# Two attention stages: units in the order D D G G D M, and the projections' steps spread over them by a table of their TensorE time

## The chip, the cores and the metric

The kernel runs on one core of a Trainium2 chip. The metric is the device time of one execution in microseconds (us); the kernel before took 2622.73 us in the median of three runs (2622.46 to 2626.35).

## The reference

Eight stages follow each other on a sequence of 512 tokens with 1024 features, all in float32: two attention blocks (`first_block`, layers 0 and 1), and then a block of four gated feed-forward stages around a state space mixer and a convolution mixer. The change touches the attention blocks only. One layer of them computes

```python
h = rms_norm(x, pre_norm[l])
proj = h @ w_in[l]     # split into dq dk dv dgate, gq gk gv ggate, mq mgate
oa = diff_attention(rope(dq), rope(dk), dv, lam)     # 6 heads, two softmaxes each: p1 - lam * p2
oa = rms_norm(oa, diff_subln[l]) * (1 - lambda_init) * silu(dgate)
ob = gqa_attention(rope(norm(gq)), rope(norm(gk)), gv) * silu(ggate)     # 6 heads on 2 key heads
mk, mv = split(rms_norm(mem, mem_norm[l]) @ w_mem_kv[l])
om = softmax(mq @ mk.T / 8) @ mv * silu(mgate)     # 4 heads on 256 memory rows
x = x + rms_norm(concat(oa, ob, om) @ w_out[l], post_norm[l])
```

## The kernel before

Every float32 product of the projections is made of three passes on TensorE (`mm3`, lines 160 to 164): high by high, high by low, low by high, where `splith` (lines 166 to 170) makes the high part by a copy on ACT and the low part by a subtraction on DVE. Weights come by DMA into a `raw` tile (line 144); `load` makes their high part on ACT (line 151) or DVE (149) and their low part on DVE or POOL (156). Of twelve weight tiles in a row, eight have their low part made on POOL and four both parts on DVE. In attention the high and low tiles are taken from a pool `w` of 13 tiles, two for each load.

**Units.** Attention itself (`attn`) is a list of 40 units. A D unit is one block of 128 queries of one differential head with its two softmaxes: 24 of them in three groups D0, D1, D2 of two heads by four blocks. A G unit is two blocks of queries of a grouped head: 12 in two groups G0, G1 of three heads by two. An M unit is a whole memory head: 4. For a unit, PE makes the scores (`unit_scores`, line 566 for D, 574 for G, 583 for M), DVE takes two maxima (line 556), ACT makes two exponentials with their sums (558), in a D unit DVE combines both softmaxes (the mix, lines 592 to 594), PE transposes the result (`unit_turn`, line 618, four matmuls for each block of queries, 606 in M), ACT copies it out as the high part (619), DVE makes the low part (`unit_low`, 624), and PE multiplies by the values (`unit_av`, 641 and 642). `unit_out` folds and stores a finished head (652 to 688).

**Steps.** The projections come in chunks. `chunk_d` makes queries, keys and values of two D heads, `chunk_g` those of three G heads, `chunk_gate` (T0 to T3) a quarter of the gates, `chunk_mkv` (KV) the memory's keys and values and `chunk_mq` (MQ) the memory queries. A chunk loads its weights and then yields in steps. A D step is 24 matmuls of 384 columns for one block of tokens, a G step 24 of 320, an MQ step 24 of 256, a step of a gate 48 of 256 (two blocks), a KV step 24 of 512. After its matmuls a D step issues the rope on DVE and POOL, two splits and, one step later, eight transposes (line 394); a G step has a norm with a square and a power on POOL (464, 186) and the lines 466, 471, 473 and 475 on DVE.

**The order around the change.** D0 is projected ahead of all units. The loop over the units (end of `attn`) issues for unit i: the scores of i + 2, the exponentials of i + 1, the low part of i - 1, the mix and transposes of i, the values of i - 1, the output of i - 2. Steps of the chunks are issued in between by three helpers: `starts(i)` issues the first half of each step whose time has come, `ends()` the other half, and `need(i)` issues whatever is left of every chunk up to one that is due. When a step's time comes is told by the list `fill` in `DEFAULT`, with a first unit and a distance in units for each chunk; the order of the groups is the string `order`. From this text a scheduler makes each engine's queue when the program is built: it may take a later instruction first where an earlier one would not be ready by its reckoning. On the chip each engine runs its queue in order.

SBUF tiles are taken from pools by name (`BUFS`, with `ALIAS`). Queries and keys (`dqk`, `gq`, `mk`, `mq`, `memT`) and the two tiles of transposed probabilities (`pt`) share the pool `u8` of six with tiles of other stages.

## Time and profile before

| | before |
|---|---|
| median of three runs | 2622.73 us (2622.46 to 2626.35) |
| the profiled execution | 2622.51 us, span 2620.7 us |
| PE busy | 2529.3 us (97%) |
| DVE, ACT, POOL busy | 1456.7 us (56%), 1045.6 us (40%), 672.3 us (26%) |
| mean granted clock of TensorE | 0.989 |
| attention, layer 0: first unit's work to the last | about 62 to 312 us |
| attention, layer 1 | about 406 to 653 us |

The span is the time from the first to the last instruction. A busy PE is not PE at its peak, since a matmul's duration covers its way through the array and the next one starts before it ends. The granted clock is 1.00 where TensorE runs at the higher of its two levels (2.4 GHz) and 0.50 where it runs at the lower (1.2 GHz). Transposes of line 618 mark the pace of the units: one block of four matmuls for a D unit, two for a G unit.

### The profile page before, as it was taken

How to read it: one execution, taken by the hardware profiler on the slowest of the kernel's cores; microseconds unless marked ns; L12 is line 12 of the kernel's file. 1: busy time of each engine (PE TensorE's matmuls, PEld its weight loads, DVE VectorE, ACT ScalarE, POOL GpSimd, SP SyncE). 2: the span in 40 equal slices, each digit the busy share in tenths (PEclk: the TensorE clock that was granted, in tenths of full speed). 3: DMA queues.
4: the chain of work that ended last, by engine and by line, in shares of the span. 5: the costliest groups of instructions: out<-in, count | busy, mean ns of one | idle time of the engine just before them, and what ended most of it. 6: DMA issues, size and time to landing. Idle time of an engine off the chain costs nothing.

```text
span 2620.7 us, 34611 instructions
## 1 busy us (share of the span) xinstructions
PE 2529.3 (97%) x13503; PEld 2180.6 (83%) x13503; DVE 1456.7 (56%) x2309; ACT 1045.6 (40%) x1964; POOL 672.3 (26%) x887
## 2 busy tenths in 40 slices
PE   7998999989999999989999999999999998999998
PEld 7997889978888788888888888888888876888887
DVE  6777667786478952488433332533323797533322
ACT  5457645576334442323433322433323434433321
POOL 5543245543135620223200000200002781300000
PEclk9999999999999999999999999999999999999999
DMA  4211142112234542543222223222222211222221
GB/s 158 67 52 61 55 155 70 61 57 79 75 102 185 189 171 104 184 162 114 97 97 97 97 98 105 96 97 97 98 98 85 98 64 41 104 90 97 101 92 65
DMA packets 68899, 262.81 MB, mean 100 GB/s; under 512 B 7936, under 2 KB 8448, under 8 KB 64384
## 3 DMA queue, kind: packets, MB, share of 16 engines
q1 hardware_dynamic: 68736, 260.61, 28.4%
q8 instruction: 106, 1.74, 0.3%
q14 instruction: 57, 0.47, 0.1%
HBM read 239.61 MB, written 20.97 MB: 99 GB/s over the span
## 4 chain that ended last, share of the span: by engine, by line
PE 50%; DVE 4%; POOL 1%; issue 1%; ACT 0%; DVEq 0%; POOLq 0%; ACTq 0%
PE t L163 16%; PE t L164 16%; PE t L162 16%; DVE t L1250 1%; POOL t L156 1%; DVE t L156 0%; DVE t L209 0%; PE t L217 0%; DVE t L241 0%; PE t L1106 0%; ACT t L203 0%; PE t L1275 0%; PE t L1105 0%; PE t L1104 0%; DVE t L170 0%
## 5 line engine op out<-in xcount | busy, mean ns | idle before, releaser
L162 PE MATMUL t<-t,t 128*128 128x512 f32 (+2 forms) x3593 | 1304.2, 365 | 12.3 <-ACT t L169 4.8
L163 PE MATMUL t<-t,t 128*128 128x512 f32 (+2 forms) x3593 | 1303.9, 363 | 6.0 <-POOL t L1229 3.4
L164 PE MATMUL t<-t,t 128*128 128x512 f32 (+2 forms) x3593 | 1302.4, 363 | 1.5 <-DVE t L170 1.3
L156 DVE TENSOR_TENSOR t<-t,t 128x1024 fp32r<-128x1024 f32 (+2 forms) x318 | 399.2, 1258 | 695.0 <-PE t L163 608.8
L162 PEld LDWEIGHTS t<-t,t 128*128 128x128 f32 x3593 | 678.4, 189 | 118.5 <-ACT t L169 9.9
L163 PEld LDWEIGHTS t<-t,t 128*128 128x128 f32 x3593 | 680.2, 189 | 108.3 <-POOL t L1229 4.2
L164 PEld LDWEIGHTS t<-t,t 128*128 128x128 f32 x3593 | 679.8, 189 | 102.0 <-DVE t L170 3.3
L151 ACT ACTIVATE t<-t 128x1024 fp32r<-128x1024 f32 (+2 forms) x370 | 386.5, 1048 | 678.5 <-PE t L164 591.5
L156 POOL TENSOR_TENSOR t<-t,t 128x512 fp32r<-128x512 f32 (+4 forms) x98 | 179.4, 1847 | 692.2 <-PE t L163 635.8
L170 DVE TENSOR_TENSOR t<-t,t 128x512 fp32r<-128x512 f32 (+3 forms) x316 | 193.6, 631 | 141.3 <-ACT t L169 140.8
L169 ACT ACTIVATE t<-t 128x512 fp32r<-128x512 f32 (+3 forms) x316 | 155.6, 517 | 249.2 <-DVE t L300 98.7
L299 ACT ACTIVATE t<-t 128x512 f32<-128x512 f32 x88 | 52.5, 597 | 217.6 <-PE t L164 215.0
L558 ACT ACTIVATE t<-t,t 128x512 f32<-128x512 f32 (+1 forms) x176 | 114.1, 658 | 37.1 <-DVE t L556 35.0
L238 POOL TENSOR_SCALAR t<-t,t 128x1 f32<-128x1 f32 x32 | 12.0, 375 | 424.8 <-ACT t L235 420.0
L556 DVE TENSOR_REDUCE t<-t 128x1 f32<-128x512 f32 (+1 forms) x160 | 106.1, 681 | 14.7 <-PE t L574 8.7
L1250 DVE SCALAR_TENSOR_TENSOR t<-t,t,t 128x512 f32<-128x512 f32 x136 | 95.5, 750 | 11.3 <-PE t L164 9.6
L624 DVE TENSOR_TENSOR t<-t,t 128x512 fp32r<-128x512 f32 x112 | 76.1, 685 | 42.0 <-ACT t L619 34.8
L1204 POOL TENSOR_TENSOR t<-t,t 128x1024 fp32r<-128x1024 f32 (+5 forms) x12 | 18.9, 1577 | 236.3 <-DVE t L170 236.3
L961 POOL TENSOR_TENSOR t<-t,t 128x64 f32<-128x64 f32 (+3 forms) x112 | 65.2, 601 | 54.6 <-DVE t L890 46.8
L209 DVE SCALAR_TENSOR_TENSOR t<-t,t,t 128x512 f32<-128x512 f32 x72 | 55.7, 815 | 40.7 <-POOL t L186 40.5
L979 DVE TENSOR_TENSOR t<-t,t 128x256 f32<-128x256 f32 x128 | 65.4, 574 | 12.7 <-DMA t<-in_s5bc 12.4
L186 POOL TENSOR_TENSOR t<-t,t 128x1 f32<-128x1 f32 (+2 forms) x98 | 69.5, 711 | 7.0
(220 smaller groups left out, 2235.5 us busy)
## 6 DMA issues: line engine op xcount, KB each, us to landing
t<-in_W SPq DMA_DIRECT2D x356, 512.0 KB, 3.5
mats<-t SPq DMA_DIRECT2D x16, 1024.0 KB, 4.9
t<-mats SPq DMA_DIRECT2D x16, 1024.0 KB, 5.5
t<-in_gv SPq DMA_DIRECT2D x19, 512.0 KB, 4.1
t<-in_W SPq DMA_DIRECT2D x24, 384.0 KB, 3.2
t<-in_W SPq DMA_DIRECT2D x8, 480.0 KB, 3.5
t<-in_x SPq DMA_DIRECT2D x4, 512.0 KB, 7.1
t<-in_mem SPq DMA_DIRECT2D x4, 512.0 KB, 3.8
```

Source lines behind the costliest of these rows:

```text
L151: nc.scalar.activation(h[:, :c], raw[:, :c], AF.Copy)
L156: eng.tensor_tensor(out=l[:, o:o + m], in0=raw[:, o:o + m], in1=h[:, o:o + m].bitcast(F32), op=ALU.subtract)
L162: mm(out, lhs[0], rhs[0], start=start, stop=False)
L163: mm(out, lhs[0], rhs[1], start=False, stop=False)
L164: mm(out, lhs[1], rhs[0], start=False, stop=stop)
L169: nc.scalar.activation(h, src, AF.Copy)
L170: nc.vector.tensor_tensor(out=l, in0=src, in1=h.bitcast(F32), op=ALU.subtract)
L186: self.nc.gpsimd.tensor_tensor(out=r, in0=r, in1=self.mh.to_broadcast([P, n]), op=ALU.pow)
L556: v.tensor_reduce(out=mx[:, q * w:q * w + w], in_=part, axis=AX.X, op=ALU.max, negate=True)
L558: act.activation(e[:, i], part[:, i - q * w], AF.Exp, bias=mx[:, i:i + 1], accum_out=u["d"][:, i:i + 1])
L624: v.tensor_tensor(out=lo, in0=tp, in1=h.bitcast(F32), op=ALU.subtract)
L1250: v.scalar_tensor_tensor(out=pc, in0=z[:, i:i + 512], scalar=cp[:, f, 5 + i:6 + i], in1=pc, op0=ALU.mult, op1=ALU.add)
```

## The change

The units go D0, D1, G0, G1, D2, M. The list `fill` is now an order of chunks, and when a step's time comes is worked out: `room` says how much TensorE time a unit of each kind leaves free, `STEPS` how many steps a chunk has and how long one is on TensorE, and a step is put at the first unit by whose end the free time exceeds the time of the steps ahead of it. T3 goes from the first place to the last. Queries and keys get a pool of their own (`a8`, five tiles), so do the two tiles `pt`, and `w` falls from 13 to 10 tiles.

```diff
-DEFAULT = {"pool": [0, 1, 3, 4, 6, 7, 9, 10], "hv": [2, 5, 8, 11], "after": [], "order": "DGDGDM", "fill": [["T3", 55.0, 2], ["T0", 8, 0.5], ["D1", 15, 1.5], ["G0", 3, 1.5], ["T1", 25.0, 2], ["G1", 4, 2], ["T2", 0, 1], ["D2", 15.0, 1], ["KV", 28.0, 1], ["MQ", 29.0, 2]]}
+DEFAULT = {"pool": [0, 1, 3, 4, 6, 7, 9, 10], "hv": [2, 5, 8, 11], "after": [], "order": "DDGGDM", "fill": "T0 D1 G0 T1 G1 T2 D2 KV MQ T3", "room": {"D": 4.1, "G": 2.5, "M": 2.5}}
+
+STEPS = {"D": (4, 4.2), "G": (4, 3.5), "T": (2, 5.8), "KV": (2, 5.5), "MQ": (4, 2.9)}
...
-    BUFS = {"u2": 6, "u4": 10, "u8": 6, "w": 13, "wf": 11, "raw": 3,
+    BUFS = {"u2": 6, "u4": 10, "u8": 6, "a8": 5, "pt": 2, "w": 10, "wf": 11, "raw": 3,
...
-    ALIAS = {k: "u4" for k in "gcs dv dst gk gst mt mv mst e gain xn xs rot cy z".split()} | {k: "u2" for k in "t1 y0 junk sg gg cb tmp su pbc pmt dbl tap".split()} | {k: "u8" for k in "dqk gq memT mk mq pt p8 mat z2 dg zz".split()}
+    ALIAS = {k: "u4" for k in "gcs dv dst gk gst mt mv mst e gain xn xs rot cy z".split()} | {k: "u2" for k in "t1 y0 junk sg gg cb tmp su pbc pmt dbl tap".split()} | {k: "u8" for k in "p8 mat z2 dg zz".split()} | {k: "a8" for k in "dqk gq memT mk mq".split()}
...
-        fill = [dict(at=max(at, start.get(nm, -1)), by=by, due=due[nm], after=start.get(nm, -1), gen=chunks[nm]) for nm, at, by in PRM["fill"]]
+        room, have = [], 0.0
+        for u in units:
+            have += PRM["room"][u["id"][0]]
+            room.append(have)
+        fill, took = [], 0.0
+        for nm in PRM["fill"].split():
+            steps, cost = STEPS[nm if nm in STEPS else nm[0]]
+            ats = []
+            for k in range(steps + 1):
+                ats.append(next((i for i in range(n) if room[i] > took), n))
+                took += cost if k < steps else 0.0
+            fill.append(dict(ats=[max(a, start.get(nm, -1)) for a in ats], due=due[nm], after=start.get(nm, -1), gen=chunks[nm]))
...
-            while fill and fill[0]["at"] <= i:
+            while fill and fill[0]["ats"][0] <= i:
                 ends()
-                if fill and fill[0]["at"] <= i:
-                    fill[0]["at"] += fill[0]["by"]
+                if fill and fill[0]["ats"][0] <= i:
+                    if len(fill[0]["ats"]) > 1:
+                        fill[0]["ats"].pop(0)
                     advance(fill[0], 0)
```

In the program's text, ahead of the scheduler, the steps move as follows. Before: T3 and T0 whole at unit 5, D1 and G0 whole at unit 6, T1, G1 and T2 at units 11 and 12, D2 at 15 to 19, KV at 28 to 30, MQ at 30 to 34. Now: T0 at units 0 to 2, D1 at 2 to 6, G0 at 6 to 10, T1 at 10 to 12, G1 at 13 to 16, T2 at 16 to 20, D2 at 21 to 26, KV at 28 to 30, MQ at 30 to 33, T3 at 33 to 36.

What the scheduler makes of it is read from the queues. A row names the line, the operation, the tile written and those read, and the size written; line numbers of the change are two higher in this part of the code. Three places of layer 0 follow.

**D0's units 6 and 7.** PE, before: the transposes of D0's unit 6 (tile 1374) with what stands behind them. Lines 162 to 164 with 320 columns are a step of G1.

```order
L163 MATMUL t_1768<-t_1712,t_63 128x320
L164 MATMUL t_1768<-t_1711,t_63 128x320
L162 MATMUL t_1768<-t_1717,t_63 128x320
L618 MATMUL t_1374<-t_64,t_845 128x128 x4
L163 MATMUL t_1768<-t_1718,t_63 128x320
L574 MATMUL t_1355<-t_1111,t_1110 128x512 x2
L574 MATMUL t_1356<-t_1111,t_1110 128x512 x2
L574 MATMUL t_1389<-t_1111,t_1110 128x512 x2
L164 MATMUL t_1768<-t_1717,t_63 128x320
L162 MATMUL t_1768<-t_1717,t_63 128x320
```

PE now: the transposes of unit 6 (tile 1011) and of unit 7 (tile 1100), which read the mix of unit 7.

```order
L166 MATMUL t_1303<-t_1043,t_63 128x320
L396 MATMUL t_988<-t_63,t_977 128x128 x4
L620 MATMUL t_1011<-t_64,t_857 128x128 x4
L568 MATMUL t_994<-t_671,t_670 128x512
L568 MATMUL t_995<-t_671,t_670 128x512
L568 MATMUL t_1060<-t_671,t_670 128x512
L568 MATMUL t_1061<-t_671,t_670 128x512
L568 MATMUL t_1130<-t_671,t_670 128x512
L620 MATMUL t_1100<-t_64,t_999 128x128 x4
L643 MATMUL t_1017<-t_459,t_214 128x256
```

DVE now, at the same place: the low part of unit 6 (line 626), then what stands ahead of the mix of unit 7 (line 596, tile 999).

```order
L626 TENSOR_TENSOR t_460<-t_1011,t_459 128x4x128
L558 TENSOR_REDUCE t_1066<-t_994 128x1
L558 TENSOR_REDUCE t_1066<-t_995 128x1
L468 TENSOR_REDUCE t_1090<-t_1084 128x4
L594 RECIPROCAL t_1095<-t_856 128x1
L558 TENSOR_REDUCE t_1136<-t_1060 128x1
L595 SCALAR_TENSOR_TENSOR t_1095<-t_856,t_1095,t_64 128x1
L558 TENSOR_REDUCE t_1136<-t_1061 128x1
L596 SCALAR_TENSOR_TENSOR t_999<-t_999,t_1095 128x512
L473 TENSOR_TENSOR t_1085<-t_1085,t_1092 128x256
```

Steps of projections stood around unit 6's transposes; now five score matmuls stand between the transposes of units 6 and 7, and eight rows of DVE between the low part of the one and the end of the mix of the other.

**G units.** PE, before, in G1's units (28 to 39 of the blocks of transposes): transposes, scores and values, with no step among them.

```order
L618 MATMUL t_2731<-t_64,t_2661 128x128 x4
L641 MATMUL t_2771<-t_459,t_1702 128x256
L574 MATMUL t_2711<-t_1701,t_1700 128x512 x2
L618 MATMUL t_2759<-t_64,t_2717 128x128 x4
L574 MATMUL t_2745<-t_1701,t_1700 128x512 x2
L618 MATMUL t_2765<-t_64,t_2717 128x128 x4
L642 MATMUL t_2771<-t_460,t_1702 128x256
```

PE now, in G1's units: a step of D2 (384 columns).

```order
L576 MATMUL t_2381<-t_1614,t_1613 128x512 x2
L165 MATMUL t_2517<-t_2303,t_63 128x384
L166 MATMUL t_2517<-t_2302,t_63 128x384
L164 MATMUL t_2517<-t_2302,t_63 128x384
L657 MATMUL t_2275<-t_64,t_2273 128x64 x4
L643 MATMUL t_2264<-t_459,t_1028 128x256
L576 MATMUL t_2445<-t_1614,t_1613 128x512 x2
L165 MATMUL t_2517<-t_2303,t_63 128x384
L576 MATMUL t_2446<-t_1614,t_1613 128x512
L620 MATMUL t_2360<-t_64,t_2244 128x128 x4
```

D2's later steps went from the second D group into the G units; they stand in one bunch of five blocks of transposes, and the blocks ahead of it and behind it have no step.

**The last D units and M.** PE, before: the last transposes of D2 (tile 3443) and M's first (line 606).

```order
L618 MATMUL t_3443<-t_64,t_3391 128x128 x4
L583 MATMUL t_3449<-t_2957,t_3134 128x256 x4
L583 MATMUL t_3450<-t_2957,t_3134 128x256 x4
L606 MATMUL t_3477<-t_64,t_3429 128x128 x4
L641 MATMUL t_3409<-t_459,t_2209 128x256
L583 MATMUL t_3489<-t_2957,t_3134 128x256 x4
```

PE now: the last transposes of D2 (tile 3391) and the start of T3's second step, 48 matmuls, all ahead of M's first transposes.

```order
L585 MATMUL t_3367<-t_2841,t_3018 128x256 x4
L620 MATMUL t_3391<-t_64,t_3312 128x128 x4
L164 MATMUL t_3397<-t_3266,t_63 128x256
L165 MATMUL t_3397<-t_3267,t_63 128x256
L166 MATMUL t_3397<-t_3266,t_63 128x256
L164 MATMUL t_3397<-t_3266,t_63 128x256
```

T3 stood ahead of T0, at the start of the stage.

## Rows read from the trace of the kernel before

**Rows 1.** Windows of the two attention stages: start:end, length, busy us (instructions) of PE, PEld, DVE, ACT, POOL, then granted clock, DMA share, GB/s.

```profile
62.00:312.00 250.00, 232.79 (x1643) 216.75 (x1641) 192.91 (x362) 157.26 (x387) 105.75 (x153) 0.98 0.19 63
406.00:653.00 247.00, 229.75 (x1593) 212.91 (x1592) 191.26 (x358) 158.95 (x388) 112.26 (x155) 0.97 0.19 66
```

**Rows 2.** The same view, cut at the groups of units (eight of layer 0, three of layer 1).

```profile
62.00:135.00 73.00, 71.04 (x526) 70.21 (x525) 54.03 (x96) 35.83 (x89) 38.18 (x50) 1.00 0.23 74
135.00:159.00 24.00, 21.66 (x146) 19.59 (x144) 15.45 (x27) 14.94 (x34) 9.12 (x12) 1.00 0.20 66
159.00:205.00 46.00, 44.17 (x314) 42.52 (x311) 42.87 (x90) 27.84 (x75) 26.08 (x36) 1.00 0.14 47
205.00:225.00 20.00, 15.87 (x102) 13.88 (x103) 15.50 (x30) 15.03 (x35) 8.64 (x16) 0.83 0.22 67
225.00:247.00 22.00, 19.84 (x141) 17.06 (x139) 17.07 (x31) 18.44 (x45) 5.54 (x9) 1.00 0.21 72
247.00:270.00 23.00, 20.75 (x113) 16.95 (x113) 18.15 (x32) 13.19 (x28) 5.09 (x8) 0.93 0.14 46
270.00:297.00 27.00, 25.00 (x199) 23.13 (x197) 20.78 (x41) 20.77 (x54) 7.39 (x14) 1.00 0.28 94
297.00:312.00 15.00, 14.48 (x117) 13.43 (x115) 9.07 (x20) 11.22 (x32) 5.71 (x10) 1.00 0.00 1
544.00:563.00 19.00, 15.65 (x99) 13.03 (x100) 14.97 (x31) 14.73 (x34) 7.82 (x13) 0.82 0.22 84
585.00:610.00 25.00, 22.98 (x120) 18.81 (x120) 18.49 (x32) 13.57 (x29) 5.09 (x8) 0.86 0.14 46
636.00:653.00 17.00, 14.82 (x103) 13.46 (x104) 9.60 (x20) 14.88 (x43) 11.12 (x15) 0.90 0.25 94
```

**Rows 3.** The same view for the transposes of line 618 alone (PE, PEld).

```profile
225.00:247.00 22.00, 6.99 (x48) 5.65 (x47) 1.00 0.21 72
```

**Rows 4.** Groups of lines on DVE, 50 to 320 us: form xcount | busy us, mean ns | idle before.

```profile
L556 DVE TENSOR_REDUCE t<-t 128x1 f32<-128x512 f32 x72 | 47.9, 681 | 10.3 <-PE t L574 6.0 <-PE t L566 4.1
L624 DVE TENSOR_TENSOR t<-t,t 128x512 fp32r<-128x512 f32 x56 | 38.0, 684 | 19.7 <-ACT t L619 16.4 <-ACT t L611 3.0
L594 DVE SCALAR_TENSOR_TENSOR t<-t,t 128x512 f32<-128x512 f32 x24 | 20.5, 854 | 0.4
L593 DVE SCALAR_TENSOR_TENSOR t<-t,t,t 128x1 f32<-128x1 f32 x24 | 5.7, 239 | 0.2
L592 DVE RECIPROCAL t<-t 128x1 f32<-128x1 f32 x24 | 3.6, 152 | 0.0
L466 DVE TENSOR_REDUCE t<-t 128x4 f32<-128x256 f32 x8 | 3.3, 409 | 1.2 <-POOL t L464 1.2
L156 DVE TENSOR_TENSOR t<-t,t 128x1024 fp32r<-128x1024 f32 x9 | 11.5, 1280 | 1.4 <-PE t L163 1.4
```

**Rows 5.** The same view on ACT.

```profile
L558 ACT ACTIVATE t<-t,t 128x512 f32<-128x512 f32 x72 | 49.5, 692 | 20.7 <-DVE t L556 19.1 <-DVE t L592 1.6
L619 ACT ACTIVATE t<-t 128x512 fp32r<-128x512 f32 x48 | 28.5, 600 | 11.6 <-PE t L618 11.5
```

**Rows 6.** Line 594 (the mix of a D unit) in the whole run: ns minimum/median/maximum.

```profile
L594 DVE SCALAR_TENSOR_TENSOR t<-t,t x48: 724/751/2295, 58.4 to 633.2; 128x512 f32<-128x512 f32 x48
```

**Rows 7.** The timeline of PE: start, us, instruction (two that follow each other).

```profile
60.32 0.28 PE L162 MATMUL t<-t,t 128*128 128x256 f32 x1
60.44 0.28 PE L163 MATMUL t<-t,t 128*128 128x256 f32 x1
```

**Rows 8.** Waits of PE from 205 to 225 us: total us, times, longest.

```profile
PE t L618 <- ACT t L558: 1.9, 1, 1.9
PE t L618 <- DVE t L624: 1.5, 1, 1.5
PE t L618 <- DVE t L664: 1.4, 1, 1.4
```

**Rows 9.** Groups of lines on POOL, 50 to 320 us.

```profile
L156 POOL TENSOR_TENSOR t<-t,t 128x1024 fp32r<-128x1024 f32 x7 | 17.4, 2492 | 0.1
```

## The prediction

> **What bounds the kernel now.** The windows of the two attention stages come first [rows 1]: in 250 us of layer 0 and 247 us of layer 1 PE is busy for 232.8 and 229.8 us, so it idles 17.2 us in each, and its granted clock averages 0.98 and 0.97. The program outside attention is the same before and after, so what the change can win lies in these two stretches. Cut at the groups of units [rows 2], the reader is to see where that idle time stands. While a pile of projection matmuls is at hand (62 to 135 us) PE idles 2.0 us of 73. It idles 2.3 us of 24 in the first G group, 1.8 us of 46 in the second D group, 4.1 us of 20 at that group's end, 2.2 us of 22 in the second G group, 2.3 us at the start of KV, 2.0 and 0.5 us in the last D group and in M. Where PE idles long its clock falls too: 0.83 from 205 to 225 us and 0.93 from 247 to 270 us in layer 0, 0.82, 0.86 and 0.90 in the three windows shown of layer 1. A clock share lost is PE time lost: 0.17 of 15.9 us is 2.7 us, 0.07 of 20.8 is 1.5, and in layer 1 0.18 of 15.7 is 2.8, 0.14 of 23.0 is 3.2, 0.10 of 14.8 is 1.5. Idle time and clock together are 34.5 + 11.7 = 46 us: more than that the change can hardly win.
>
> Next, what ends the idle time. From 205 to 225 us the waits are those of the transposes of line 618, for an exponential on ACT and for line 624 and 664 on DVE [rows 8]. At that place the PE queue has no projection matmul left, and the units run at the pace of their chain: scores, two maxima on DVE, two exponentials on ACT, in a D unit the mix on DVE, the transposes, the copy on ACT, the low part on DVE. The group costs of that chain are the rows on DVE and ACT [rows 4, 5].
>
> **The change, part by part.** The instructions stay the same; their order and three pool sizes change. So the sum is of waits that go and waits that come, and each is taken from a stretch of the trace in which units run with or without steps beside them.
>
> *The hole at the end of the second D group goes.* In the old order the steps of G1, T2 and D2 are used up when the last units of D1 are at work, and 4.1 us of idle time and 2.7 us of clock are lost there; in layer 1 it is 19 - 15.65 = 3.35 and 2.8 us [rows 2]. In the new order the second D group ends beside G1 and T2, whose matmuls stand around its last transposes. Both holes go: -13.0 us. Nothing worse than before can be hidden in that term, since what is late next at this place is PE itself.
>
> *G units.* Without steps beside them, 225 to 247 us, 48 transposes [rows 3] are 6 G units (8 each), and they lose 2.16 us of idle time, 0.36 a unit. In the old order both G groups lose 2.34 + 2.16 = 4.5 us. In the new order of PE, 9 of the 12 G units still have no projection matmul between their transposes: the scheduler takes T2 and D2 in two bunches, early and around the ninth unit. So 9 x 0.36 = 3.2 us stay, and 1.3 us a layer go: -2.5 us for both.
>
> *D units: new waits.* Here the change costs. D0 and D1 now follow each other, with T0, D1, G0, T1 and G1 beside them. At two places of the new order PE has next to nothing between the transposes of two D units. The first is shown above: between the transposes of D0's units 6 and 7 stand five score matmuls. DVE has to do, from the low part of unit 6 to the mix of unit 7, line 624 (0.684), four maxima (4 x 0.681), line 466 (0.409), the two small ones (0.152 and 0.239) and the mix (0.854): 5.06 us [rows 4]. Ahead of the low part go four transposes (6.99 / 48 = 0.146 each, 0.58 us [rows 3]) and the copy on ACT (0.600 [rows 5]). From transposes to transposes that is 6.2 us. PE's own work in it is the transposes and five score matmuls of 512 columns. Two 256-column matmuls start 0.12 us apart [rows 7], so I estimate 0.24 us for 512 columns and 1.8 us in all. PE waits 6.2 - 1.8 = 4.4 us. The second place, before unit 14, has the same list with a second line 466 and a sum of squares of about that size (5.9 us), less work of PE (transposes, two pairs of score matmuls, eight matmuls of line 641 and 642, four of line 655: some 2.9 us): 7.1 - 2.9 = 4.2 us. Around units 2 and 8 the same count leaves 0.8 and 0.5 us. So 10 us a layer come, and the 2.0 + 1.8 = 3.8 us that the two D groups lose now go with their old order: +6.2 us a layer, taken twice +12.5 us. The ends of this term: nothing at all (DVE runs ahead, and PE finds its work done: -3.8 x 2 = -7.6 us), and DVE slowed, which is the rival below.
>
> *T3 moves from the pile into the last D group.* Its 96 matmuls (4 blocks of rows, 8 slices, 3 products) are 96 x 0.12 = 11.5 us of PE [rows 7]. In the old order they stand ahead of T0, where PE is busy throughout, so they cost 11.5 us there; in the new order they stand beside D2's last units and before M's second unit. That stretch loses 2.0 + 0.5 us now, and in layer 1 2.2 us of idle time and 1.5 us of clock in its M part alone [rows 2]. Of these 6.2 us I take 5 to be filled, as M's last units still have nothing beside them: -5 us. Its ends are 0 and -6.2.
>
> *KV's start.* PE waits there for the norm of the memory (lines 203 to 217), which stays. Its clock loss, 1.5 and 3.2 us, follows on the lean stretch ahead; with D2's steps nearer I take 2 us of 4.7 as gone: -2 us, between 0 and -4.7.
>
> *Pools.* Weight buffers fall from 13 to 10 tiles (5 pairs). Where a chunk of 4 pairs follows another, only one pair is loaded ahead, and the next waits for its copy and its subtraction: 1.28 us on DVE, 2.49 us on POOL [rows 4, 9]. Units' matmuls and the last step of the chunk in front (24 x 0.12 us and more) stand beside it, so I take 0. If the cover is gone, the nine changes of chunk cost up to 2.49 us each where POOL does it. SP only issues the loads earlier or later; three raw buffers are unchanged. The separate pool for queries and keys has five tiles, and five is what D0, D1 and G0 hold at once, so I take 0 there.
>
> **Sum.** -13.0 - 2.5 + 12.5 - 5 - 2 = -10 us. The profiled execution took 2622.5 us, 0.2 us under the median of the three runs; the forecast is **2613 us**, with 2605 to 2621 as the forecast's own range from the ends of the last two terms and some us at either side for the count of the new waits.
>
> **A rule that speaks against it.** The mix reads two tiles in SBUF. It takes 0.751 us in the median and up to 2.295 us [rows 6], and POOL's subtractions of weights, 2.49 us each [rows 9], run beside the D units. The Trainium skill, page "SBUF — State Buffer", section "SBUF: two separate sides", says that a DVE operation with two SBUF inputs and a GpSimd operation exclude each other for a whole instruction. The longest mix agrees with that [rows 6]; by the rule alone each of the 9 subtractions that POOL makes in the new D groups of a layer could hold up a mix, and the sum would turn positive.
>
> **The rivals.**
>
> *All of it wins.* If the new waits in the D groups do not come (DVE does the maxima before the transposes need them), the term of +12.5 becomes -7.6, and the sum is -30 us: 2592. For it: from 62 to 135 us D units with steps beside them lose only 2.0 us. Against it: DVE was busy for 54 of 73 us there and for 42.9 of 46 from 159 to 205 us [rows 2], so it has little to run ahead with. 0.22.
>
> *Slower: POOL holds up the mix.* 9 of the 14 weight tiles of T0, D1, G0, T1 and G1 have their subtraction on POOL. If 8 of them in a layer meet a mix of the 16 D units, and each makes it 2.295 instead of 0.854 us, that is 8 x 1.44 = 11.5 us on the path from unit to unit, 23 us in both layers: -10 + 23 = +13, 2636 us. It decides once more than 4 mixes of a layer are hit where PE has no step to put beside them. For it: two D groups in a row with steps all through. Against it: the mean of the mix, 0.854, is only 0.1 us over its median, so about one in fifteen is hit now. 0.17.
>
> *No change.* The holes go, but as much comes back: the scheduler fills PE's queue with whatever is ready, in either order, so idle time only moves. Then -13.0 against +12.5 and the rest near nothing: 2622. For it: the bunches in the new order are as dense as in the old. Against it: T3's 11.5 us do move to a leaner place. 0.16.
>
> **The numbers.** The forecast has 0.45, of which 0.33 are faster by over 0.2%, 0.11 within it and 0.01 slower; 0.2% (5 us) is about what a measurement of this kernel can tell from no change. With the first rival faster has 0.55; with 0.12 of "no change", the same has 0.23; with the second rival and the 0.04 left of the third, slower has 0.22. The range reaches from the first rival to the second, 2592 to 2636 us; the few us beyond for weight buffers and for still slower mixes are the part left out.
>
> **What would show it.** In the profile after: the window at the end of the second D group has no low clock, and its waits for line 624 are gone (first term); PE waits some 4 us each for DVE ahead of line 620's transposes twice in the D groups of each layer (third term); M's and the last D group's windows idle less (fourth). Wrong would be: a D stretch whose idle time is below 4 us a layer (first rival), or mixes at 2 us in numbers (second).

## The result, and the profile of the changed kernel

The changed kernel takes **2660.45 us** in the median of four runs (2659.98 to 2665.21), the kernel before 2624.54 (2622.46 to 2627.53): a ratio of 1.0139, 95% interval 1.0124 to 1.0154. It is slower by some 36 us. The forecast was 2613 us with a range of 2592 to 2636: the sign was wrong and the time lies outside the range. The profiled execution of the changed kernel took 2665.2 us, the longest of the four, and that of the kernel before 2622.5; so the two traces differ by 42.7 us, some 7 more than the medians, and that much of what follows is the scatter of single executions.

| | before | after |
|---|---|---|
| span of the profiled execution | 2620.7 us | 2663.4 us |
| PE busy | 2529.3 us | 2545.0 us |
| DVE, ACT, POOL busy | 1456.7, 1045.6, 672.3 us | 1457.2, 1043.2, 672.5 us |
| mean granted clock | 0.989 | 0.980 |

DVE, ACT and POOL did the same work in the same time. PE is busy 16 us longer for the same matmuls (the lower clock) and idle 27 us longer. Line numbers of the changed kernel are two higher than before in this part.

The windows of the changed kernel, cut at its groups of units (columns as in [rows 1]): of layer 0, D0 and D1 from 64 to 180 us in five pieces, G0 and most of G1 to 226, the end of G1 to 251, the start of KV to 275, D2 to 311, M to 326; then the same ten of layer 1.

```profile
64.00:104.00 40.00, 39.03 (x257) 37.13 (x255) 28.67 (x59) 24.03 (x58) 21.50 (x28) 0.96 0.15 47
104.00:120.00 16.00, 9.96 (x48) 8.14 (x47) 13.32 (x28) 6.31 (x19) 7.39 (x12) 0.68 0.26 92
120.00:150.00 30.00, 30.00 (x229) 29.36 (x227) 23.06 (x47) 16.30 (x43) 17.30 (x26) 1.00 0.09 27
150.00:173.00 23.00, 17.67 (x115) 15.17 (x115) 18.25 (x41) 10.54 (x31) 17.80 (x27) 0.93 0.18 63
173.00:180.00 7.00, 7.00 (x58) 6.78 (x57) 4.08 (x10) 6.35 (x17) 3.23 (x5) 1.00 0.01 2
180.00:226.00 46.00, 43.46 (x289) 39.99 (x287) 31.02 (x57) 29.12 (x71) 13.78 (x17) 1.00 0.10 34
226.00:251.00 25.00, 19.05 (x131) 16.47 (x130) 16.76 (x30) 15.20 (x35) 6.32 (x7) 0.86 0.40 140
251.00:275.00 24.00, 21.31 (x120) 17.71 (x119) 18.12 (x31) 14.48 (x31) 9.24 (x10) 0.93 0.08 26
275.00:311.00 36.00, 34.55 (x292) 34.08 (x291) 25.09 (x43) 23.76 (x63) 6.84 (x15) 1.00 0.21 72
311.00:326.00 15.00, 13.73 (x108) 12.41 (x107) 9.83 (x21) 10.37 (x24) 5.66 (x9) 1.00 0.29 106
...
425.00:466.00 41.00, 37.44 (x257) 35.90 (x256) 30.73 (x57) 23.24 (x56) 18.58 (x26) 1.00 0.15 54
466.00:479.00 13.00, 8.73 (x49) 7.32 (x48) 10.74 (x26) 6.87 (x19) 9.32 (x13) 0.87 0.34 113
479.00:510.00 31.00, 31.00 (x238) 30.49 (x237) 23.42 (x50) 17.73 (x48) 19.54 (x28) 1.00 0.09 27
510.00:535.00 25.00, 18.41 (x114) 15.91 (x113) 17.06 (x41) 9.55 (x28) 16.27 (x25) 0.86 0.17 56
535.00:541.00 6.00, 6.00 (x49) 5.80 (x48) 3.90 (x10) 4.98 (x14) 3.22 (x5) 1.00 0.02 4
541.00:588.00 47.00, 44.48 (x297) 40.99 (x296) 31.41 (x57) 29.48 (x70) 12.39 (x16) 1.00 0.08 29
588.00:614.00 26.00, 19.25 (x126) 17.27 (x126) 16.31 (x29) 16.26 (x36) 5.52 (x8) 0.80 0.37 133
614.00:636.00 22.00, 19.49 (x113) 15.97 (x112) 17.63 (x29) 13.01 (x29) 8.43 (x10) 1.00 0.00 1
636.00:675.00 39.00, 36.98 (x298) 36.24 (x297) 26.07 (x46) 24.91 (x64) 7.72 (x15) 0.96 0.23 82
675.00:690.00 15.00, 14.14 (x114) 13.04 (x113) 10.32 (x21) 10.52 (x24) 5.49 (x9) 1.00 0.30 107
```

Read each row as the prediction did: length less PE's busy time is idle time, one minus the clock times the busy time is what the clock lost. The steps were meant to be even, and PE's queue is not: from 120 to 150 us PE has no gap at all, on either side of it PE idles 6.0 us of 16 at a clock of 0.68 and 5.3 of 23 at 0.93. The two D groups lose 18.3 us in layer 0 (2.5, 9.2, 0, 6.6, 0) and 18.1 in layer 1 (3.6, 5.4, 0, 9.2, 0). The second place is new as well: the end of G1 (226 to 251 and 588 to 614 us) loses 8.6 and 10.6 us, where the second G group lost about 2 [rows 2].

As to length, layer 0 takes 264 us (62 to 326) against 250, layer 1 takes 266 (424 to 690) against 247, the stretch between them 98 against 94, and what follows 1973.4 against 1967.7.

What PE waited for, in the two D groups of layer 0 (62 to 180 us; total, times, longest), and then what DVE waited for from 62 to 323 us:

```profile
PE t L620 <- DVE t L596: 5.2, 2, 3.2
PE t L568 <- DVE t L626: 1.6, 1, 1.6
...
DVE t L151 <- PE t L165: 5.4, 1, 5.4
DVE t L424 <- PE t L166: 4.8, 1, 4.8
```

The first row is the wait the prediction had named: PE ahead of the transposes, for the mix, at units 7 and 14 (3.2 and 2.0 us). In layer 1's D groups it comes once, 2.0 us. In the last two rows DVE itself stands idle at the head of its queue, with work of a step that waits for PE's projection matmuls: the cast of a weight tile ahead of unit 7, and the rope at 187 us, in G0. Before, the cast waited 0.5 us at most in layer 0, and the rope 1.2 us, in layer 1 3.2. The timeline around unit 7 shows both sides (start, us, instruction, idle time before it and what ended it):

```profile
103.63 0.63 PE L620 MATMUL t<-t,t 128*128 128x128 f32 x4
104.67 1.19 PE L568 MATMUL t<-t,t 128*128 128x512 f32 x4 [0.40 <-ACT t L397]
107.44 0.50 PE L568 MATMUL t<-t,t 128*128 128x512 f32 x1 [1.59 <-DVE t L626]
111.10 1.08 PE L620 MATMUL t<-t,t 128*128 128x128 f32 x4 [3.16 <-DVE t L596]
...
115.32 0.41 PE L164 MATMUL t<-t,t 128*128 128x256 f32 x1
115.53 0.41 PE L165 MATMUL t<-t,t 128*128 128x256 f32 x1
...
102.51 1.84 DVE L151 CAST t<-t 128x960 fp32r<-128x960 f32 x1 [5.39 <-PE t L165]
104.46 2.33 DVE L158 TENSOR_TENSOR t<-t,t 128x960 fp32r<-128x960 f32 x1
106.71 0.68 DVE L626 TENSOR_TENSOR t<-t,t 128x512 fp32r<-128x512 f32 x1
107.31 1.27 DVE L558 TENSOR_REDUCE t<-t 128x1 f32<-128x512 f32 x2
110.22 0.74 DVE L596 SCALAR_TENSOR_TENSOR t<-t,t 128x512 f32<-128x512 f32 x1
...
101.57 2.27 POOL L158 TENSOR_TENSOR t<-t,t 128x960 fp32r<-128x960 f32 x1 [3.01 <-ACT t L153]
104.21 1.57 POOL L158 TENSOR_TENSOR t<-t,t 128x640 fp32r<-128x640 f32 x1 [0.37 <-ACT t L153]
```

PE ends its run of projection matmuls at 103.5 us; DVE has waited 5.4 us for that run, and then has a cast and a subtraction of weights to do (102.51 to 106.8) before the low part of unit 6, the maxima and the mix of unit 7. In that time PE has five score matmuls. The two engines take turns instead of working side by side. Behind the wait PE's matmuls of 256 columns start 0.21 us apart (115.32 and 115.53), before 0.12 [rows 7]: the granted clock stands at its lower level there.

### The profile page after: what moved, and what is told of

Read it like the earlier page. It is cut to its first block, busy times and chain, and to the rows that moved or that the text cites. A ratio compares the mean times of both kernels' runs of the same rounds, so it can differ in the third digit from the quotient of the medians.

```text
span 2663.4 us, 34476 instructions
## 1 busy us (share of the span) xinstructions
PE 2545.0 (96%) x13503; PEld 2192.0 (82%) x13503; DVE 1457.2 (55%) x2309; ACT 1043.2 (39%) x1964; POOL 672.5 (25%) x887
## 4 chain that ended last, share of the span: by engine, by line
PE 49%; DVE 3%; POOL 1%; issue 1%; ACT 0%; DVEq 0%; POOLq 0%; ACTq 0%
PE t L165 16%; PE t L166 16%; PE t L164 16%; DVE t L1265 1%; POOL t L158 1%; DVE t L211 0%; DVE t L158 0%; PE t L219 0%; DVE t L243 0%; DVE t L1088 0%; PE t L1290 0%; DVE t L172 0%; ACT t L205 0%; DVE t L1093 0%; PE t L1274 0%
## 5 line engine op out<-in xcount | busy, mean ns | idle before, releaser
L164 PE MATMUL t<-t,t 128*128 128x512 f32 (+3 forms) x3593 | 1309.5, 366 | 19.0 <-ACT t L171 6.4
L165 PE MATMUL t<-t,t 128*128 128x512 f32 (+3 forms) x3593 | 1307.9, 364 | 5.9 <-POOL t L1244 3.1
L166 PE MATMUL t<-t,t 128*128 128x512 f32 (+3 forms) x3593 | 1305.2, 364 | 1.4 <-DVE t L172 1.3
L172 DVE TENSOR_TENSOR t<-t,t 128x512 fp32r<-128x512 f32 (+3 forms) x316 | 203.0, 659 | 144.4 <-ACT t L171 144.0
L1265 DVE SCALAR_TENSOR_TENSOR t<-t,t,t 128x512 f32<-128x512 f32 x136 | 95.7, 753 | 13.1 <-PE t L166 11.4
L302 DVE TENSOR_TENSOR t<-t,t 128x512 f32<-128x512 f32 x88 | 60.0, 682 | 31.9 <-PE t L166 29.1
L643 PE MATMUL t<-t,t 128*128 128x256 f32 x224 | 65.4, 311 | 9.6 <-ACT t L621 9.0
L621 ACT ACTIVATE t<-t 128x512 fp32r<-128x512 f32 x96 | 57.4, 599 | 43.3 <-PE t L620 42.2
```

The costliest lines, as they stand in the source:

```text
L164: mm(out, lhs[0], rhs[0], start=start, stop=False)
L165: mm(out, lhs[0], rhs[1], start=False, stop=False)
L166: mm(out, lhs[1], rhs[0], start=False, stop=stop)
L172: nc.vector.tensor_tensor(out=l, in0=src, in1=h.bitcast(F32), op=ALU.subtract)
L643: mm(acc[:, c], vs, pth[:, kp, c], start=(kt == 0), stop=False)
L1265: v.scalar_tensor_tensor(out=pc, in0=z[:, i:i + 512], scalar=cp[:, f, 5 + i:6 + i], in1=pc, op0=ALU.mult, op1=ALU.add)
```

## The experiments

All numbers are medians with the ratio to the kernel before as it ran beside each, since its median moved between 2624.3 and 2626.8; differences in us are differences of ratios times 2624.5. An interval is about 0.1 to 0.17% to either side, 2 to 4.5 us, so that a difference of two runs is known to some 4 to 6 us. The first theory was A (the even spreading costs), with B (the order) and C (the weight pool) as rivals.

**e1_pools.** The pools alone: the changed lines `BUFS` and `ALIAS` in the kernel before.

> The kernel before with the pools of the change alone (a8 of five tiles, pt of two, w 10 instead of 13); old order of units, old list of steps. Theory A (the even spreading of the steps costs: the changed kernel takes 36 us more because PE has no stock of projection matmuls to work on while DVE makes the mix of a D unit): the pools alone cost under 5 us, 2620 to 2630 us. Theory B (the order D D G G costs: sixteen D units in a row are too much for DVE, whatever the steps do): the same, 2620 to 2630. Theory C (the smaller weight pool costs: steps wait for their weights): most of the 36 us is here, 2640 us or more.

2616.5 us, ratio 0.9962 (0.995 to 0.9975): 10 us *faster* than before. C falls, and a gain appears that no theory had.

**e2_order.** `"order": "DDGGDM"` in the kernel before, nothing else.

> The kernel before with the order D D G G D M alone: the old list of steps (T3 and T0 early, then D1, G0 and so on in bunches), the old pools. Theory A (spreading): with the steps in bunches the new order costs little, 2615 to 2632 us. Theory B (order): 2645 us or more. Theory C (weight pool): as with A, 2615 to 2632, since w stays at 13.

2628.4 us, ratio 1.0015 (1.0006 to 1.0024). B falls for the listed steps.

**e3_even_old.** In the changed kernel:

```diff
-"order": "DDGGDM", "fill": "T0 D1 G0 T1 G1 T2 D2 KV MQ T3"
+"order": "DGDGDM", "fill": "T0 G0 D1 T1 G1 T2 D2 KV MQ T3"
```

> The changed kernel with the old order D G D G D M: steps spread evenly by their TensorE time (G0 now ahead of D1 in the list, as its group comes first; T3 last), the pools of the change. Theory A (spreading): 2645 us or more, as the spreading stays. Theory B (order): 2615 to 2632. Theory C (weight pool): 2645 or more.

2642.8 us, ratio 1.0067 (1.0052 to 1.0082). Between the expectations, nearer to A: about half of the loss is there with the old order.

**e4_w12.** `"w": 12` instead of 10 in the changed kernel.

> The changed kernel with 12 weight tiles instead of 10, nothing else. Theory A (spreading) and theory B (order): within 6 us of the changed kernel, 2654 to 2667 us. Theory C (weight pool): one pair more is loaded ahead, so at least 10 us less, 2650 us or under.

2659.5 us, ratio 1.0133 (1.0118 to 1.0148): no difference that can be told. C is out.

**e5_orderpools, e7_t3last_new, e8_t3last_old** take T3 apart from the rest: the list of steps of the kernel before, with the new pools, in new or old order; e7 and e8 have T3 at the list's end:

```diff
-"fill": [["T3", 55.0, 2], ["T0", 8, 0.5], ... ["MQ", 29.0, 2]]
+"fill": [["T0", 8, 0.5], ... ["MQ", 29.0, 2], ["T3", 33, 2]]
```

> The kernel before with the new order and the new pools, and the old list of steps; only the even spreading (with T3 last) is then missing from the change. The pools alone took 8.7 us off, the order alone put 3.8 us on. Theory A (the spreading costs, order and pools add up): 2615 to 2626 us, so that the spreading with T3's move is worth about +40 us. Theory D (order and pools help or harm only together, as the queries and keys of three chunks want the new pool in the new order): under 2612, or over 2640 if they harm each other.

> New order, new pools, the old list of steps, but T3 at the end of the list (at unit 33, as in the change) instead of at its head. Theory A (the spreading of the other steps costs): 2610 to 2630 us; by the prediction's term T3's move saves about 5 us against the same kernel with T3 first. Theory E (T3's move takes the stock away from D0): 15 us or more above the same kernel with T3 first.

> Old order, new pools, the old list of steps with T3 at its end instead of at its head. The same with T3 first took 2616.5 us. By the prediction's term (T3's 11.5 us fill the idle time of the last D group and of M): 2608 to 2613 us. Theory E (T3's move takes work from D0's first units): 2625 us or more.

e5: 2629.2 us, ratio 1.0015 (1.0006 to 1.0024), between the expectations and 3 us above A's. e7: 2641.0, 1.0063 (1.0048 to 1.0078), short of the 15 us of theory E, far from a gain. e8: 2633.0, 1.0036 (1.0022 to 1.005), against 0.9962 with T3 first (e1). Moving T3 from the head of the list to its end *costs* 13 us in the new order and 19 in the old, where the prediction had a gain of 5. The windows of D0's first units, first of e1 (T3 first), then of e8 (T3 last):

```profile
62.00:127.00 65.00, 65.00 (x480) 64.25 (x478) 48.98 (x91) 36.26 (x87) 39.66 (x50) 1.00 0.24 78
...
62.00:127.00 65.00, 59.70 (x413) 56.74 (x412) 48.52 (x95) 33.81 (x87) 35.12 (x49) 0.97 0.18 58
```

With T3 there PE has no gap in 65 us; without it PE idles 5.3 us and the clock falls to 0.97. PE was full in that stretch *because* of T3's matmuls. At the other end they do fill: from the first unit of D2 to the end of M, both layers, e8 loses 7.6 us and e1 14.8. The head costs more than the end gains.

**e6_room6.** In the changed kernel, every step earlier:

```diff
-"room": {"D": 4.1, "G": 2.5, "M": 2.5}
+"room": {"D": 6.0, "G": 3.6, "M": 3.6}
```

> The changed kernel with room 6.0, 3.6, 3.6 instead of 4.1, 2.5, 2.5: the same order, pools and sequence of chunks, each step put about a third of the way earlier, so that PE has steps in hand while a D unit waits for DVE. Theory A (PE lacks a stock of steps in the D groups): at least 12 us less than the change, 2648 us or under, with less idle time in the first two D groups. Theory E (it is T3's move to the end that takes the stock away from D0's first units, and the pace matters little): within 6 us of the change, 2654 to 2667.

2667.7 us, ratio 1.0166 (1.0151 to 1.0181): slower, against both (above theory E's bound by 1 us). So "PE lacks a stock" is not the cause in this simple form. That steps which come earlier also bring their own work on DVE earlier is a likely reason, not a tested one.

**e9_nodve_change, e10_nodve_pools, e11_t3first_change.** e9 in the changed kernel, e10 in e1; e11 only puts T3 at the head of the changed kernel's `fill`:

```diff
-"pool": [0, 1, 3, 4, 6, 7, 9, 10], "hv": [2, 5, 8, 11]
+"pool": [0, 1, 2, 3, 4, 5, 6, 7, 8, 9, 10, 11], "hv": []
```

> The changed kernel with the weights' high parts all on ACT and their low parts all on POOL, so that no cast and no subtraction of weights stands in DVE's queue in attention (before, four tiles of twelve have both on DVE). In the trace of the change the longest idle times of DVE in the first two D groups are waits for PE at the head of its queue (5.4 us at line 151, 4.8 at line 424), and PE then waits for what stands behind. Theory F (the weight work at the head of DVE's queue is what makes the D units late in the spread order): at least 10 us less than the change, 2650 us or under, and more than the same edit brings in the kernel with the old order and list. Theory G (it is the missing work of PE at units 7 and 14, and whatever DVE does the maxima and the mix take 5 us there): within 6 us of the change, or as much as the same edit brings there. Theory H (POOL's subtractions hold up DVE, the prediction's slower rival): slower than the change by 5 us or more, as POOL has half as many again.

> The control to the run before: old order, old list, new pools (2616.5 us) with the weights' parts on ACT and POOL only. Theory F: within 5 us of 2616.5, since DVE's queue is hidden by the pile of projections. Theory G: the same shift as in the changed kernel. Theory H: slower by some us, but less than in the changed kernel.

> The changed kernel with T3 at the head of the list of chunks instead of its end; the planner then puts every other step 11.6 us of room later. With the old list, T3's move to the end cost 11.8 us in the new order and 16.5 in the old. If that price is the cover that T3's matmuls give to D0's first units, it comes back here: 2643 to 2652 us. If the spread order loses the cover all the same, as only the first step falls to unit 0: 2655 us or more.

e9: 2647.5 us, ratio 1.0083 (1.0068 to 1.0098), 15 us less than the change. e10: 2623.3, 0.9989 (0.998 to 0.9998), 7 us *more* than e1, where theory F had allowed 5; some 4 of the 7 us between the two traces lie behind attention, where the order of PE is the same in both. By the totals that is theory F. The traces refute its mechanism. The two D groups of each layer, the change first, then e9 (windows from about the first transposes of unit 0 to those of the first G unit):

```profile
62.00:180.00 118.00, 105.66 (x709) 98.55 (x708) 89.38 (x186) 64.98 (x169) 67.62 (x97) 0.93 0.15 51
424.00:541.00 117.00, 102.58 (x704) 96.39 (x703) 86.81 (x183) 62.84 (x164) 67.39 (x97) 0.96 0.16 53
...
60.00:176.00 116.00, 102.69 (x692) 95.31 (x691) 80.55 (x172) 66.80 (x169) 71.15 (x99) 0.93 0.16 49
412.00:528.00 116.00, 102.53 (x697) 95.29 (x696) 79.70 (x172) 66.89 (x170) 71.96 (x99) 0.94 0.16 49
```

With no weight work on DVE the D groups lose 20.5 and 19.6 us of idle time and clock, with it 19.7 and 18.5. From transposes to transposes they last 115.7 and 115.2 us, with it 115.9 and 116.3. PE waits elsewhere instead (3.6 us at line 164 for line 626, in each layer). The 4.8 us of line 424 that the expectation names lie in G0, not in the D groups. What e9 gains lies in the G groups (68.0 us each instead of 71.3 and 72.9) and in the projections ahead of each layer's first unit (8 us in the two together). The weight work that stands ahead of unit 7 in DVE's queue is therefore not what makes the D groups long. H falls too: with half as many subtractions again on POOL the D groups are no longer than in the change. e11: 2640.7, 1.006 (1.0043 to 1.0077): T3 at the head gives 21 us back, a little more than expected.

**e12_t1head**, a try at a better kernel: e1 with T1 in T3's place at the head and `["T3", 19, 2]` ahead of KV.

> A try at a kernel better than both: old order, old list, new pools, with T1 at the head in T3's place (as large, so D0's first units keep their cover) and T3 between D2 and KV, started at units 19 and 21, where the end of the second D group, the second G group and KV's start lose 17 us in layer 0 of the kernel with the new pools. If the hole takes the 11.6 us of T3 as other work would: 2600 to 2610 us. If the hole is only moved (the scheduler takes T3 early): 2612 to 2620.

2622.8 us, ratio 0.9987 (0.9978 to 0.9996), 7 us worse than e1 and beyond both expectations. D0 keeps its cover (PE is busy for 64.2 of 65 us from 62 to 127), but nothing is won in attention, and 5 of the 7 us between the two traces lie behind it.

**e13_best_spread.** The changed kernel with T3 first, no weight work on DVE, and `"w": 12`.

> The changed kernel with three edits at once: T3 at the head of the list (alone worth -19.8 us), no weight work on DVE in attention (alone -13.0), w 12 instead of 10 (alone -1.0). Theory I (two separate causes: D0's first units lost T3's matmuls as cover, and weight work stands ahead of the mix in DVE's queue): the savings add up, 2623 to 2631 us, that is about the list in the same order. Theory J (one cause, waits of the D units for DVE, which either edit takes away): about as T3 alone, 2636 to 2643 us.

2642.2 us, ratio 1.0074 (1.0059 to 1.0089): the total is theory J's, nothing on top of e11. J's one cause is not borne out: the first two D groups take 112.5 us in each layer, in e11 107.2 and 111.7, although no weight work is left on DVE. Its D units 7 to 12 (window, then waits of DVE and PE there) show the same taking of turns with another instruction at the head:

```profile
106.00:149.00 43.00, 33.46 (x198) 30.06 (x196) 30.63 (x60) 20.52 (x51) 21.21 (x32) 0.76 0.10 31
...
DVE t L558 <- PE t L568: 6.0, 2, 4.9
...
PE t L620 <- DVE t L594: 3.2, 1, 3.2
```

**e14_w10.** The kernel before with `"w": 10`, nothing else.

> The kernel before with 10 weight tiles instead of 13 and nothing else. The three new pools together took 8.7 us off. If that is the separate pool of queries, keys and pt: 2622 to 2632 us here (no gain, or a loss from fewer weights ahead). If the fewer weight tiles themselves reorder the program for the better: 2612 to 2620.

2617.6 us, ratio 0.997 (0.9961 to 0.998). This program has the same queues as e1 on every engine: the separate pools of queries, keys and `pt` change nothing in the old order, and the whole gain is the smaller weight pool. That e1 and e14 are 1.1 us apart is the scatter of one program.

**e15_kv18, e16_kv24.** e1 with KV begun at unit 18, or 24, instead of 28.

> A try at a better kernel: old order, old list, new pools, with the memory's keys and values (KV, 48 matmuls of 512 columns) begun at unit 18 instead of 28. In the order of PE its matmuls then stand at the end of the second D group (block 26 of the transposes), where the kernel with the new pools loses 6.8 and 10.7 us in the two layers, and not at blocks 41 and 42, where it loses 6.2 and 3.4. If the hole is filled and the old place loses nothing: 2600 to 2608 us. If the wait for the memory's norm moves along with KV: 2612 to 2620.

> The same with KV begun at unit 24: its matmuls then stand in the second G group (blocks 34 to 36), whose units without steps lose 4.5 and 5.1 us. The hole at the end of the second D group stays. If G units with steps lose nothing and the old place of KV loses nothing: 2604 to 2610 us; if the norm's wait moves along: 2613 to 2620.

2629.8 us, ratio 1.0023 (1.0013 to 1.0032), and 2622.2, 0.9992 (0.9982 to 1.0001): 16 and 8 us worse than e1. In e15 the wait for the memory's norm comes along (waits of PE from 186 to 246 us):

```profile
PE t L217 <- DVE t L209: 3.6, 1, 3.6
```

In e16 attention itself came out no longer: M's last transposes in layer 1 begin at 639.3 us, in e1 at 642.2. The rest of the program then took 1981.8 us to the end of the span against 1973.5, though PE's order is the same in both from 712 us on; so its loss lies behind attention, and why is open. e15 and e16 are both beyond their expectations.

**e17_even_old_t3first** has `"order": "DGDGDM"` and `"fill": "T3 T0 G0 D1 T1 G1 T2 D2 KV MQ"` in the changed kernel; **e18_w8** has `"w": 8` in the kernel before.

> The one corner that is missing of order (old, new), T3 (first, last) and steps (listed, even), all with 10 weight tiles: old order, T3 first, steps spread evenly. The old order with T3 last and even steps took 2642.8 us, with T3 first and the list 2616.5. If the even spreading costs about 10 us in either order once T3 stands first: 2623 to 2630 us. If T3's place is the whole cost in the old order: 2614 to 2620. If the spreading costs as much here as with T3 last, or T3's place matters nothing: 2635 us or more.

> The kernel before with 8 weight tiles instead of 13, nothing else. With 10 it took 2617.6 us against 2624.4. Theory K (fewer weights ahead keep the weights' casts and subtractions out of the way of D0's units, and the fewer the better): 2605 to 2615 us. Theory L (10 happened to give a good order; with 8, four pairs, the next chunk's weights come late): 2620 us or more.

e17: 2660.3 us, ratio 1.0136 (1.0121 to 1.0151), beyond what any theory expected: with T3 and T0 first, the steps of G0 and D1 stand together among D0's last units, and PE waits for the splits that the transposes of their queries and keys (line 396) need (window, then waits of PE, 80 to 111 us):

```profile
80.00:111.00 31.00, 22.70 (x150) 21.61 (x149) 20.34 (x40) 10.18 (x30) 22.51 (x32) 0.92 0.17 49
...
PE t L396 <- DVE t L172: 7.2, 2, 4.0
```

e18: 2627.5 us, ratio 1.0012 (1.0003 to 1.0022): theory L; ten tiles are a good place, not a direction.

**All eight corners**, with ten weight tiles throughout, as the ratio to the kernel before:

| order | list, T3 first | list, T3 last | even, T3 first | even, T3 last |
|---|---|---|---|---|
| D G D G D M | 0.9962 (e1) | 1.0036 (e8) | 1.0136 (e17) | 1.0067 (e3) |
| D D G G D M | 1.0015 (e5) | 1.0063 (e7) | 1.0060 (e11) | 1.0139 (the change) |

Even spreading costs in each of the four pairs: 46, 8, 12 and 20 us. The order costs 14, 7 and 19 us and gains 20 in the pair with even steps and T3 first. T3's place costs 19, 13 and 21 us and gains 18 in one. Only the spreading has one sign. The best of the eight, e1 (or e14, one number changed), beats both kernels. Two things are mixed into the table: with even steps and the old order G0 stands ahead of D1 in the list of chunks (e3, e17), and with even steps T3 at the head also puts every other step later. And the 7 and 8 us are not far outside their intervals.

Where the spreading costs is seen in the pair with the new order and T3 last. In e7 the two D groups of the layers, cut as above, lose 12.7 and 7.8 us, in the change 19.7 and 18.5:

```profile
61.00:158.00 97.00, 88.73 (x585) 80.98 (x584) 80.84 (x154) 56.51 (x144) 53.03 (x78) 0.95 0.19 58
415.00:507.00 92.00, 85.88 (x597) 80.57 (x595) 77.19 (x152) 56.29 (x143) 54.61 (x77) 0.98 0.21 66
```

That is 18 us, about the 20 that the runs differ by.

## Why the prediction was wrong

**The hole at the end of the second D group, -13.0.** In its own place it is gone as part of the D units' count below. The failing sentence is "Nothing worse than before can be hidden in that term, since what is late next at this place is PE itself". The steps still run out ahead of KV, only elsewhere: from 226 to 251 us, at the end of G1, PE has no projection matmul, and that end loses 8.6 and 10.6 us.

**G units, -2.5.** The 46 and 47 us of G units ahead of that end lose 2.5 us each, near the 3.2 us a layer that the forecast left standing. With the end, G units lose 24.3 us in both layers instead of 9.0: +15.3 where -2.5 stood. Taken together, the hole and the G units lost 22.0 us and now lose 24.3: the hole was moved, not closed, and the 15.5 us of these two terms did not come.

**D units, +12.5.** The mechanism and the two places were right in layer 0: PE waits ahead of the transposes for the mix at units 7 and 14; layer 1 has one such wait. The size was not. The two groups lose 18.3 and 18.1 us, not 10 a layer; less the 3.8 a layer that the term took off, +28.8 instead of +12.5. The larger part of what is missing is the clock. The term priced the idle time of the new waits and put their clock at nothing, though the prediction had read from the kernel before that the clock falls where PE idles long. Idle time came to 12.3 and 14.4 us, the clock cost another 6.0 and 3.7: behind the wait at unit 7 it is 0.68 from 104 to 120 us, and the matmuls of the next step run at the lower level. The smaller part is waits that the count left out. At unit 7 the list of DVE's work began at the low part of unit 6 (5.06 us; measured 4.25, from 106.71 to 110.96). What stood *ahead* of the low part, a cast and a subtraction of weights that waited for PE, was not in it: from transposes to transposes it took 7.5 us (103.63 to 111.10), not 6.2. By e9 that weight work does not set the length of the D groups, so listing it would not have mended the term; other waits take its place.

**T3, -5.** The step "PE is busy throughout, so they cost 11.5 us there" took the cover for a cost. Without T3's matmuls D0's units have PE waiting (e8). At the other end the last D group and M still lose 2.7 and 4.4 us. The 6.2 us that were to be filled left out layer 1's last D group, which lost 2.6 us before:

```profile
610.00:636.00 26.00, 23.41 (x187) 21.72 (x185) 19.27 (x39) 19.16 (x46) 7.21 (x13) 1.00 0.22 78
```

With it the end went from 8.8 to 7.1 us, -1.7 where -5 stood. Measured alone, the move costs 13 to 21 us in three settings of four and gains 18 in the fourth.

**KV, -2.** The sum is right (-2.2), in part by luck: 4.2 and 2.5 us are lost at its start now, 3.7 and 5.2 before [rows 2], so all of it came in layer 1.

**Pools, 0.** Right for queries, keys and `pt` (e14 has e1's queues). Wrong for `w`: in the old order 10 tiles instead of 13 gain 8 to 10 us (e14, e1). In the changed kernel 12 or 10 make no difference (e4).

Corrected, the terms come to -13.0 + 15.3 + 28.8 - 1.7 - 2.2 = +27 us; the stretch between the layers adds 4 (PE waits 4.4 us there for a split ahead of line 396) and what follows 5.7. That is 37 of the 42.7 us between the two traces; the rest is not accounted for. Of the 5.7 us at the end 4 lie where the order of PE is the same before and after (from 717 and 756 us on); that stretch varies from profile to profile by as much (e16 above), and was not followed further.

**The rivals.** "All wins" is refuted by 12.3 and 14.4 us of idle time in the D groups. "POOL holds up the mix" named the right sign and the wrong mechanism: the mix of the changed kernel takes 0.751 us in the median and 1.158 at most, before up to 2.295 [rows 6], and with half as many subtractions again on POOL the D groups are no longer (e9).

```profile
L596 DVE SCALAR_TENSOR_TENSOR t<-t,t x48: 733/751/1158, 60.9 to 663.5; 128x512 f32<-128x512 f32 x48
L595 DVE SCALAR_TENSOR_TENSOR t<-t,t,t x48: 204/214/2192, 60.2 to 663.2; 128x1 f32<-128x1 f32 x48
```

"No change" had the best sentence: the scheduler fills PE's queue with whatever is ready, and idle time only moves. It was right on the bunches (PE is full from 120 to 150 us, and waits on both sides) and on the hole, which came back in G1, and wrong that what comes back in all equals what goes.

**What is shown and what is argued.** Shown: each part's price in the table of corners; that T3's matmuls were D0's cover; that the spreading's cost lies in the D groups where T3 is last and the order new; that PE and DVE wait for each other in turn at unit 7; that DVE's weight work is not what makes the D groups long. Argued only: that this taking of turns, with other work of the steps at the head of DVE's queue, is the cost of the spreading. e13 speaks for waits that move from head to head (with weight work gone, DVE's longest wait is for scores, 4.9 us), but no run took the rest of the steps' work on DVE out of the D units. So which work of DVE the D groups wait for stays open. Why the corner e17 is so much worse than its neighbours is seen in its waits for line 172, not tested.

## What to carry to other kernels

A stretch in which PE never waits is not a place where its matmuls are paid in full: ask what PE would have done there without them, before you count their removal as a gain. A wait is priced from the queue of the engine that is waited for, and with the clock that PE loses behind it, not only with the idle time. A total that comes out as a theory said does not show its mechanism: look in the trace whether the gain lies where the theory puts it (e9). And when a scheduler makes the queues, local terms don't add: here, with the steps spread, the order and T3's place change sign with each other, so a change of several parts is best measured at its corners.

## What was not expected of the hardware

A small operation can wait for a whole one of POOL. In e6 the [128 x 1] operation of line 595, 0.214 us in the median, took 2.15 us beside a subtraction of weights (DVE, then POOL):

```profile
118.49 2.15 DVE L595 SCALAR_TENSOR_TENSOR t<-t,t,t 128x1 f32<-128x1 f32 x1
...
118.24 2.39 POOL L158 TENSOR_TENSOR t<-t,t 128x1024 fp32r<-128x1024 f32 x1
```

It ends as POOL's ends, at 120.63 us. The Trainium skill, page "SBUF — State Buffer", section "SBUF: two separate sides", calls this an exclusive lock for a whole instruction, and the trace agrees. The cast of line 151, which has one input, is held up as well: 0.684 us in the median and 2.871 at most, over forms of 640 to 1024 columns; before, 0.789 and 2.895:

```profile
L151 DVE CAST t<-t x22: 488/684/2871, 15.0 to 631.2; 128x1024 fp32r<-128x1024 f32 x10, 128x768 fp32r<-128x768 f32 x8, 128x960 fp32r<-128x960 f32 x3, 128x640 fp32r<-128x640 f32 x1
```

At unit 7 of the changed kernel (timeline above) the cast ends 0.5 us after POOL's subtraction, at 104.35 us, and DVE's subtraction then takes 2.33 us beside POOL's next one, where one of the same size without POOL beside it took 1.13 before (at 78.17 us). By the median of the cast and that row I estimate 2.4 us that POOL adds ahead of the mix for which PE waits. The kernel before has longer casts of this kind, 2.69 us at 73.02 and 2.90 at 95.26, in a stretch where PE has steps at hand and idles 2.0 us of 73 [rows 2]. It does not explain the difference between the kernels: in e9 neither stands in DVE's queue, and the D groups are as long. The other surprise is the weight pool: a smaller pool makes the program faster without a single instruction less, by the other order that the scheduler then makes (e14).
